# A hybrid attention layer on one core: sums of the mix and scalings of the first attention taken from GpSimd, and the residual loaded in four steps

## The chip, the cores and the metric

The program runs on one core of one Trainium2 chip. The metric is device time in microseconds (us) of one execution, the median of several runs. One execution of each kernel was taken by the hardware profiler as well. Its engines are PE (TensorE: matmuls, with PEld its weight loads), DVE (VectorE), ACT (ScalarE), POOL (GpSimd) and SP (which here only issues DMAs).

## The reference

One decoder layer for 512 tokens of width 1024, in float32. Two attentions run side by side on the same normed input and are mixed by gates; a convolutional gated MLP and a per-layer embedding follow.

```
h = rmsnorm(x); qa, ka, va, cq, ckv, kr, gates = split(h @ w_in)
ya = swa_attention(rope(qa), rope(ka), va, sinks)        # 8 heads, window 128
yb = mla_attention(...)                                  # 8 heads, dense causal
gate_a, gate_b = split(sigmoid(gates + b_gate))
mixed = gate_a * (ya @ w_branch_a) + gate_b * (yb @ w_branch_b)
x = x + rmsnorm(mixed @ w_out)
u_gate, u_val = split(causal_dwconv(rmsnorm(x) @ w_up))  # 2 x 2816 wide
x = x + rmsnorm((gelu(u_gate) * u_val) @ w_down)
x = x + sigmoid(rmsnorm(x) @ w_ple_gate) * (p @ w_ple)

# swa_attention, per block of 128 queries:
pr = exp(s - m) / (sum(exp(s - m)) + exp(sink - m));  out = pr @ v
```

## The kernel before

Every product is made of three matmuls on rounded halves of its operands: `split` (L71) writes a high part on ACT (`whi`, L72) and the rest on DVE (`wlo`, L73), and `mm3` (L75) multiplies high by high, high by low and low by high. A weight chunk of 128x1024 is thus loaded by SP's DMA queue into `wraw`, split on ACT and DVE, and used by PE (all matmuls carry line 56). PE has to wait for `whi` and `wlo` when these two engines are late.

The work goes in stages; times are those of the trace. Projections of the input (0 to 84 us); the first attention, in eight steps of a query block n and a head group g (`swa_scores` L493, `swa_pt` L527, `swa_pv` L549; to about 160); the second attention (`mla_scores` L562 and on; to about 250); the product with the first branch's weights (`psba`, 203 to 234); the mix, a loop over eight feature blocks m (L662 to L676; 248 to 279); w_out (`yo`) with its norm `post_norm` (L724); the up projection with the convolution (`pu`; 320 to 562); the down projection in two loops; the embedding and the last gate (`pe`, `pg`; 671 to 734). While the attentions run, `fill` (L479) puts matmuls of the gate projection (`psg`) between their steps, so that PE has work.

In one step of the first attention DVE takes the masked scores and their maximum out of PSUM, ACT takes four exponentials with their sums (`sw`, L518), DVE makes the reciprocal of the denominators (`den`, L522), POOL multiplies the whole step's `sw` by them in one instruction (L524), and PE transposes the result (`ptw`), which ACT and DVE split (`pwh`, `pwl`) for the product with v (`pvw`).

In the mix the four operations after the matmuls `pb` are

```
dve.scalar_tensor_tensor(ta, gb, 1.0, pb, ALU.add, ALU.mult)                # L673
pool.tensor_tensor(ta, ta, ga[:, m, :], ALU.add)                            # L674
act.activation(mxh[:, m, :], ta, AF.Copy, scale=0.5)                        # L675
dve.scalar_tensor_tensor(mxl[:, m, :], ta, 0.5, f32(mxh[:, m, :]), ...)     # L676
```

where `ta` is a block of the tile `gx` and `mxh`, `mxl` are the halves that `yo` uses.

The down projection takes 7 products for 8 blocks. The first loop (L899) over 11 chunks c fills `M1`, `M5`, `M7` and `M6`; `drain` (L936) sums them into `U`, `V12` (a part of a tile `T`) and `C22`; the second loop (L951) reloads half of each weight chunk, splits it, subtracts it from `T2[c]` (L958) for later, and goes on with `M1` and, one chunk behind, `M3`. Then `M4` uses the split `T2`. Before `drain`, POOL's queue loads the gain (`loadgain` L658) and the residual `xn` from DRAM in four parts of 512 KB (`load` L880, issued at L881); the `post_norm` of the MLP adds it at L736.

The program's order on each engine is made by a scheduler from the order in the code and priorities; `hot` (high priority) lifts a part of the code. Each engine then runs its instructions in that fixed order.

Of the kernel before, what the change touches and what calls it, by code (L numbers as in the profile page):

```python
# [8 lines left out]
F32 = mybir.dt.float32  # L9
F32R = mybir.dt.float32r  # L10
I32 = mybir.dt.int32
AF = mybir.ActivationFunctionType
ALU = mybir.AluOpType
PSUM = bass.MemoryType.PSUM

P = 128
S = 512
NB = 4
D = 1024
# [18 lines left out]
def hybrid_kernel(ctx, tc, T):  # L38
    nc = tc.nc
    act, dve, pool = nc.scalar, nc.vector, nc.gpsimd  # L40
    order = mybir.DependencyInfo(mybir.DependencyClass.NoSync, mybir.DependencyReason.DATA)

    class pe:
# [19 lines left out]
    def opened(**kw):  # L63
        cm = tc.tile_pool(reuse_waits="tile", **kw)
        p = cm.__enter__()
        return p, lambda: cm.__exit__(None, None, None)
# [38 lines left out]
    xp, close_xp = opened(name="xp", bufs=1, side="left")  # L105
# [6 lines left out]
    qkp, close_qkp = opened(name="qkp", bufs=1, side="right")  # L112
# [48 lines left out]
    def work(name="wkt"):  # L161
        return wk.tile([P, 1280], F32, name=name, tag="wkt", bufs=3)

    xh = xp.tile([P, 8, S], F32R, name="xh", tag="xh")
# [192 lines left out]
    qT = qkp.tile([P, 8, S], F32, name="qT", tag="qT")[:96]  # L357
# [10 lines left out]
    for n in range(NB):  # L368
        ps = scT("psqp")
        b = slice(n * P, (n + 1) * P)  # L370
        for k in range(2):
            w = slice(k * 256, (k + 1) * 256)
# [34 lines left out]
    ga = gap.tile([P, 8, S], F32, name="ga", tag="ga")  # L407
    gx = []

    def gate(m):  # L410
        return ga[:, m, :] if m < 8 else gx[(m - 8) // 3][:, (m - 8) % 3, :S]
# [29 lines left out]
    kT = qkp.tile([P, 8, S], F32, name="kT", tag="kT")[:96]  # L441
# [25 lines left out]
    def latent_kr():  # L467
# [4 lines left out]
        for h in range(1, 8):  # L472
# [4 lines left out]
                     e=latent_kr).get(t, lambda t=t: gates((int(t),)))() for t in ORDER.split()]  # L477
# [15 lines left out]
    def swa_scores(n, g):  # L493
        K = 256 if n else 128
        ks = slice(max(0, n - 1) * P, (n + 1) * P)
        mk = mswa if n else mswa[:, P:]
        b = slice(n * P, (n + 1) * P)
        s = work("sw")
        m, nm, sums, es = small("m"), small("nm"), small("sums"), small("es")
        for half in range(2):  # L500
            sc = scT("sc")
            for u in range(2):
                h = 4 * g + 2 * half + u
                o = sc[:, u * K:(u + 1) * K]
                pe.matmul(o, St[:, h, b], kh[:, g, ks], start=True, stop=False)
                pe.matmul(o, St[:, h, b], kl[:, g, ks], start=False, stop=True)
            for u in range(2):
                i = 2 * half + u
                h = 4 * g + i
                o = sc[:, u * K:(u + 1) * K]  # L510
                dve.tensor_tensor_reduce(
                    out=s[:, i * K:(i + 1) * K], in0=o, in1=mk, scale=0.125, scalar=sink[:, h:h + 1],
                    op0=ALU.add, op1=ALU.max, accum_out=m[:, i:i + 1])
        dve.tensor_scalar(nm, m, -1.0, None, ALU.mult)
        dve.tensor_tensor(es, sink[:, 4 * g:4 * g + 4], nm, ALU.add)
        for i in range(4):
            w = slice(i * K, (i + 1) * K)
            act.activation(s[:, w], s[:, w], AF.Exp, bias=nm[:, i:i + 1], accum_out=sums[:, i:i + 1])  # L518
        act.activation(es, es, AF.Exp)
        den = small("den")  # L520
        dve.tensor_tensor(den, sums, es, ALU.add)
        dve.reciprocal(den, den)  # L522
        sv = s[:, :4 * K].rearrange("p (i w) -> p i w", i=4)
        pool.tensor_tensor(sv, sv, den.unsqueeze(2).to_broadcast([P, 4, K]), ALU.mult)  # L524
        return s

    def swa_pt(n, g, s):  # L527
# [135 lines left out]
    for m in range(8):  # L663
        gb = gate(8 + m)
        if m % 2 == 0:
            ch_b = chunk(T["wbb"][m // 2])
        hi, lo = ch_b
        pb = p3[m]("pb")
        for k in range(4):
            w = slice((m % 2) * S + k * P, (m % 2) * S + (k + 1) * P)  # L670
            mm3(pb, hi[:, w], lo[:, w], ybT[0][:, k, :], ybT[1][:, k, :], k == 0, k == 3)
        ta = gb
        dve.scalar_tensor_tensor(ta, gb, 1.0, pb, ALU.add, ALU.mult)  # L673
        pool.tensor_tensor(ta, ta, ga[:, m, :], ALU.add)  # L674
        act.activation(mxh[:, m, :], ta, AF.Copy, scale=0.5)  # L675
        dve.scalar_tensor_tensor(mxl[:, m, :], ta, 0.5, f32(mxh[:, m, :]), ALU.mult, ALU.subtract)  # L676
    for f in (close_ca, close_wk, close_gap, close_sp, close_cqp, close_kvp, close_yp):
# [4 lines left out]
             raw=0, hi=0, lo=0)  # L682
# [75 lines left out]
    wx = [qkp.tile([P, 4, 1024], F32R, name="wx" + t, tag=t) for t in ("kT", "qT")]  # L758
# [14 lines left out]
    xd = [dp.tile([P, D], F32, name=f"xd{n}", tag=f"xd{n}") for n in range(NB)]  # L773
# [103 lines left out]

    loads = []

    def load(dst, src):  # L880
        i = pool.dma_start(dst, src).ins  # L881
        if loads:
            tc.add_manual_dep(i, loads[-1], order, reason="load order")
        loads.append(i.name)
# [4 lines left out]
    T2 = [T2t[c // 8][:, c % 8] for c in range(NC)]  # L889
    T13 = [T2t[1][:, 4 + 2 * i:6 + 2 * i].rearrange("p a t -> p (a t)") for i in range(2)]  # L890
    B1, B2 = slice(0, S), slice(S, 2 * S)
# [35 lines left out]
    open_res()  # L927
    xn = res["xn"]
    g_post = loadgain(T["mlp_post"], load, 1)
    for n in range(NB):  # L930
        load(xn[:, n, :], xd[n])
    Ut = vp.tile([P, 2, S], F32, name="U")
    C22t = ck.tile([P, 2, S], F32, name="C22", tag="t", bufs=3)
    U, C22 = ([t[:, b] for b in range(2)] for t in (Ut, C22t))
# [2 lines left out]
    def drain():  # L937
        for b in range(2):
            act.activation(U[b], M["M1"][b], AF.Copy)
            dve.tensor_tensor(U[b], M["M6"][b], U[b], ALU.add)  # L940
        for b in range(2):
            dve.tensor_tensor(V12[b], M["M5"][b], U[b], ALU.add)
            dve.tensor_tensor(U[b], M["M7"][b], U[b], ALU.add)
            dve.tensor_tensor(C22[b], M["M5"][b], U[b], ALU.add)
# [8 lines left out]
    for c in range(NC):  # L953
        raw = wtile("raw", F32)
        nc.sync.dma_start(raw, T["wd"][2 * c + 1])
        h, l = wtile("hi", F32R), wtile("lo", F32R)
        split(h, l, raw)
        dve.tensor_tensor(T2[c], raw[:, B1], T2[c], ALU.subtract)  # L958
        for b in range(2):
            t = slice(b * P, (b + 1) * P)  # L960
            lh, ll = p1[c][:, 0, 0, t], p1[c][:, 1, 0, t]
            for x, y in ((lh, h), (lh, l), (ll, h)):
                pe.matmul(M["M1"][b], x, y[:, B1], start=False, stop=c == NC - 1 and x is ll, skip_group_check=True)
        if late:
            m3(*late)
        late = (c, (h[:, B2], l[:, B2]))
# [6 lines left out]
    for c in range(NC):  # L973
        if c % 2 == 0:
            h, l = wtile("hi", F32R), wtile("lo", F32R)
        w = slice(c % 2 * S, (c % 2 + 1) * S)
# [3 lines left out]
    ph, pl = lA[:, 0:2], lA[:, 2:4]  # L980
    wpt = xp.tile([P, 4, D], F32R, name="wpt", tag="xl")
    wph, wpl = wpt[:, 0:2, :], wpt[:, 2:4, :]
    e = xp.tile([P, NB, D], F32, name="e", tag="xh")
    raw = wtile("raw", F32)
    nc.sync.dma_start(raw, T["pT"].rearrange("p a b -> p (a b)"))
    split(ph.rearrange("p a b -> p (a b)"), pl.rearrange("p a b -> p (a b)"), raw)
    for k in range(2):
        raw = wtile("raw", F32)
# [7 lines left out]
    for n in range(NB):  # L996
        b = slice(n * P, (n + 1) * P)
        for half in range(2):
            ps = bank(3 * (n % 2), "pe")
            w = slice(half * S, (half + 1) * S)  # L1000
# [5 lines left out]
        to_hT(n, xn[:, n, :], 1 + n // 2)  # L1006
    gp = lambda k: pp[:, PP_PLE + k:PP_PLE + k + 1]
    cg = [chunk(T["wpg"][k], g=gp(k)) for k in range(4)]
    wx = [qkp.tile([P, 4, 1024], F32R, name="wy" + t, tag=t) for t in ("kT", "qT")]
    cg += [chunk(T["wpg"][4 + k], g=gp(4 + k), dst=[t[:, k, :] for t in wx]) for k in range(4)]  # L1010
    lB = fp.tile([P, 4, S], F32, name="lB", tag="fB")
    outs = [0]
# [146 lines left out]
```

## Time and profile before

| | |
|---|---|
| time, median of 3 runs | 736.94 us (735.46 to 739.03) |
| time of the profiled execution | 735.66 us |
| its span, first to last instruction | 733.9 us |
| granted TensorE clock, mean | 1.000 |
| moved from and to HBM | 85.46 and 12.85 MB |

The span leaves 1.76 us of the profiled time outside. Of the views, the shares of busy time tell which engine is full, the waits tell what an engine waited for and how long, the chain shows the work that ended last followed back in time, and the timeline lists instructions with the idle time before them.

### The profile page before, as it was taken

To read this page: it belongs to the slowest core of one execution; us is meant where nothing else is said; L and a number is where in the kernel's file an instruction comes from. 1 tells how busy PE (TensorE), PEld (TensorE's weight loads), DVE (VectorE), ACT (ScalarE), POOL (GpSimd) and SP (SyncE) were. 2 spreads that over 40 slices of the span, in tenths; PEclk is the share of its full clock that TensorE was granted. 3 is DMA by queue.
4 is the path that set the end of the run, shared out by engine and by line. 5 is a ranking of instruction groups with operands and counts; after the bars stand their busy time and mean duration, and the time that the engine had idled before them with its cause. 6 is when DMAs were issued, how large, how long until landed. Compare 5 with 4: busy or idle time off the path is not lost.

```text
span 733.9 us, 9541 instructions
## 1 busy us (share of the span) xinstructions
PE 722.6 (98%) x3496; PEld 602.6 (82%) x3496; DVE 529.0 (72%) x935; ACT 363.3 (50%) x634; POOL 83.2 (11%) x99
## 2 busy tenths in 40 slices
PE   9999999999999999999999999999999999999997
PEld 9988877788778877899888888888888888788886
DVE  6567789986777486675777676687777987789632
ACT  5833577854553334446444443544544534268521
POOL 0104022100000062210000000000000322201000
PEclk9999999999999999999999999999999999999999
DMA  9611221112112226443434324334323798945111
GB/s 321 239 42 65 62 72 59 58 58 86 58 57 75 77 88 261 190 173 101 159 129 141 125 107 156 133 132 155 123 78 129 272 322 270 373 128 169 58 59 57
DMA packets 30814, 99.38 MB, mean 135 GB/s; under 512 B 4112, under 2 KB 5392, under 8 KB 30768
## 3 DMA queue, kind: packets, MB, share of 16 engines
q1 hardware_dynamic: 24960, 76.36, 31.4%
q0 software_dynamic: 5520, 22.02, 8.3%
q8 instruction: 27, 0.44, 0.3%
q10 hardware_dynamic: 288, 0.39, 0.2%
q14 instruction: 19, 0.16, 0.1%
HBM read 85.46 MB, written 12.85 MB: 134 GB/s over the span
## 4 chain that ended last, share of the span: by engine, by line
PE 90%; DVE 7%; issue 1%; DMA 1%; ACT 0%; DVEq 0%
PE pu L56 30%; PE M L56 13%; PE psg L56 11%; PE pg L56 6%; PE yo L56 5%; PE puh L56 3%; PE psba L56 3%; PE psA L56 3%; PE psB L56 2%; PE psC L56 2%; PE scm L56 2%; PE pe L56 2%; PE pb L56 1%; DVE wlo L73 1%; PE pvm L56 1%
## 5 line engine op out<-in xcount | busy, mean ns | idle before, releaser
L56 PE MATMUL pu<-hT,whi 128*128 128x512 f32 x640 | 197.0, 389 | 0.0
L72 ACT ACTIVATE whi<-wraw 128x1024 fp32r<-128x1024 f32 (+4 forms) x105 | 102.5, 976 | 168.0 <-PE pu L56 75.6
L73 DVE TENSOR_TENSOR wlo<-wraw,whi 128x1024 fp32r<-128x1024 f32 (+2 forms) x99 | 114.5, 1160 | 64.3 <-ACT whi L72 60.9
L56 PEld LDWEIGHTS pu<-hT,whi 128*128 128x128 f32 x640 | 120.1, 188 | 25.0
L56 PE MATMUL pu<-hT,wlo 128*128 128x512 f32 x320 | 124.5, 389 | 0.0
L56 PEld LDWEIGHTS pu<-hT,wlo 128*128 128x128 f32 x320 | 60.1, 188 | 12.4
L56 PE MATMUL psg<-xh,whi 128*128 128x512 f32 x128 | 51.1, 399 | 1.3 <-DVE ga L426 0.9
L56 PE MATMUL psg<-xl,whi 128*128 128x512 f32 x128 | 50.9, 398 | 0.0
L56 PE MATMUL psg<-xh,wlo 128*128 128x512 f32 x128 | 50.8, 397 | 0.0
L832 ACT ACTIVATE cv<-pu,pp 128x512 f32<-128x512 f32 x40 | 30.6, 765 | 9.1 <-PE pu L56 9.1
L72 ACT ACTIVATE whi<-T 128x512 fp32r<-128x512 f32 (+1 forms) x32 | 23.4, 761 | 21.2 <-DVE T L909 7.8
L833 DVE SCALAR_TENSOR_TENSOR cv<-pu,pp,cv 128x511 f32<-128x511 f32 x40 | 29.8, 746 | 3.1 <-ACT cv L832 3.1
L834 DVE SCALAR_TENSOR_TENSOR cv<-pu,pp,cv 128x510 f32<-128x510 f32 x40 | 29.9, 746 | 1.1
L674 POOL TENSOR_TENSOR gx<-gx,ga 128x512 f32<-128x512 f32 x8 | 15.3, 1929 | 132.7 <-DVE gx L673 132.7
L56 PEld LDWEIGHTS psg<-xh,whi 128*128 128x128 f32 x128 | 24.0, 188 | 7.1 <-DVE ga L426 1.1
L835 ACT ACTIVATE cv<-cv 128x512 f32<-128x512 f32 x22 | 13.9, 633 | 31.9 <-DVE cv L834 31.8
L73 DVE TENSOR_TENSOR wlo<-T,whi 128x512 fp32r<-128x512 f32 (+1 forms) x32 | 26.3, 851 | 3.3 <-ACT whi L72 3.3
L815 POOL DMA_DIRECT2D dd<-f2h x11 | 6.0, 546 | 198.7 <-ACT f2h L812 198.7
L56 PEld LDWEIGHTS psg<-xl,whi 128*128 128x128 f32 x128 | 24.1, 188 | 4.8 <-issue 0.2
L56 PEld LDWEIGHTS psg<-xh,wlo 128*128 128x128 f32 x128 | 24.1, 188 | 4.7
L56 PE MATMUL puh<-hT,whi 128*128 128x256 f32 x128 | 23.8, 285 | 0.1
L582 ACT ACTIVATE sm<-sm,nm 128x512 f32<-128x512 f32 (+3 forms) x32 | 17.6, 552 | 12.4 <-DVE nm L579 12.4
(324 smaller groups left out, 1640.8 us busy)
## 6 DMA issues: line engine op xcount, KB each, us to landing
wraw<-in_wup SPq DMA_DIRECT2D x44, 512.0 KB, 3.4
wraw<-in_wd SPq DMA_DIRECT2D x22, 512.0 KB, 4.3
wraw<-in_wg SPq DMA_DIRECT2D x16, 512.0 KB, 3.4
dd<-f2h POOLq DMA_DIRECT2D x11, 384.0 KB, 2.9
dd<-X POOLq DMA_DIRECT2D x11, 384.0 KB, 2.6
wraw<-in_wo SPq DMA_DIRECT2D x8, 512.0 KB, 3.6
wraw<-in_wpg SPq DMA_DIRECT2D x8, 512.0 KB, 3.8
wraw<-in_wd SPq DMA_DIRECT2D x11, 256.0 KB, 5.2
```

Source lines behind the costliest of these rows:

```text
L56: pe.chain(out, nc.tensor.matmul(out, *a, **k))
L72: act.activation(hi, src, AF.Copy)
L73: dve.tensor_tensor(lo, src, f32(hi), ALU.subtract)
L582: act.activation(s[:, w], s[:, w], AF.Exp, bias=nm[:, n:n + 1], accum_out=sums[:, n:n + 1])
L674: pool.tensor_tensor(ta, ta, ga[:, m, :], ALU.add)
L815: pool.dma_start(dd[c][:, i], f32(v))
L832: act.activation(c, u, AF.Identity, scale=w2, bias=cb)
L833: dve.scalar_tensor_tensor(c[:, 1:], u[:, :S - 1], w1, c[:, 1:], ALU.mult, ALU.add)
L834: dve.scalar_tensor_tensor(c[:, 2:], u[:, :S - 2], w0, c[:, 2:], ALU.mult, ALU.add)
L835: act.activation(cs[0], cs[0], AF.Gelu_apprx_tanh)
```

## The change

Five edits.

1. In `swa_scores` the one multiplication on POOL becomes four, one for each head of the group: two on ACT (Copy with a scale) and two on DVE.
2. In the mix the addition on POOL goes to DVE.
3. `drain` keeps its first half (the sums into `U` of `M1` and `M6`); the six other sums are written as `drain_rest`, called in the second loop at c = 2.
4. The four loads of `xn` no longer stand ahead of `drain`; each waits for the subtraction `T2[c]` of c = 2, 4, 6 and 8.
5. The tile `e` of the embedding moves to another buffer ("kT" for "xh"), and a half of the last gate's split weights takes "xh" in its place.

```
+    wait = mybir.DependencyInfo(mybir.DependencyClass.Sync, mybir.DependencyReason.DATA)
...
-        sv = s[:, :4 * K].rearrange("p (i w) -> p i w", i=4)
-        pool.tensor_tensor(sv, sv, den.unsqueeze(2).to_broadcast([P, 4, K]), ALU.mult)
+        for i in range(4):
+            w = slice(i * K, (i + 1) * K)
+            if i < 2:
+                act.activation(s[:, w], s[:, w], AF.Copy, scale=den[:, i:i + 1])
+            else:
+                dve.tensor_scalar(s[:, w], s[:, w], den[:, i:i + 1], None, ALU.mult)
...
-        pool.tensor_tensor(ta, ta, ga[:, m, :], ALU.add)
+        dve.tensor_tensor(ta, ta, ga[:, m, :], ALU.add)
...
-    def load(dst, src):
+    def load(dst, src, after=None):
         i = pool.dma_start(dst, src).ins
+        if after is not None:
+            tc.add_manual_dep(i, after, wait, reason="load pace")
...
-    for n in range(NB):
-        load(xn[:, n, :], xd[n])
...
             act.activation(U[b], M["M1"][b], AF.Copy)
             dve.tensor_tensor(U[b], M["M6"][b], U[b], ALU.add)
+
+    def drain_rest():
         for b in range(2):
             dve.tensor_tensor(V12[b], M["M5"][b], U[b], ALU.add)
             dve.tensor_tensor(U[b], M["M7"][b], U[b], ALU.add)
             dve.tensor_tensor(C22[b], M["M5"][b], U[b], ALU.add)
...
-        dve.tensor_tensor(T2[c], raw[:, B1], T2[c], ALU.subtract)
+        t4 = dve.tensor_tensor(T2[c], raw[:, B1], T2[c], ALU.subtract).ins.name
+        if c == 2:
+            drain_rest()
+        if c in (2, 4, 6, 8):
+            load(xn[:, c // 2 - 1, :], xd[c // 2 - 1], t4)
...
-    e = xp.tile([P, NB, D], F32, name="e", tag="xh")
+    e = qkp.tile([P, NB, D], F32, name="e", tag="kT")
...
-    wx = [qkp.tile([P, 4, 1024], F32R, name="wy" + t, tag=t) for t in ("kT", "qT")]
+    wx = [p.tile([P, 4, 1024], F32R, name="wy" + t, tag=t) for p, t in ((xp, "xh"), (qkp, "qT"))]
```

The orders below are those of the built programs. After the change the code stands some lines lower: L673, L676 and L73 of before are L678, L681 and L74.

DVE in the mix, before:

```order
L673 SCALAR_TENSOR_TENSOR gx_1630<-gx_1630,pb 128x512 x2
L73 TENSOR_TENSOR wlo<-wraw,whi 128x1024
L673 SCALAR_TENSOR_TENSOR gx_1630<-gx_1630,pb 128x512
L673 SCALAR_TENSOR_TENSOR gx_1631<-gx_1631,pb 128x512
L73 TENSOR_TENSOR wlo<-wraw,whi 128x1024
L676 SCALAR_TENSOR_TENSOR mxl<-gx_1630,mxh 128x512 x2
L673 SCALAR_TENSOR_TENSOR gx_1631<-gx_1631,pb 128x512
L676 SCALAR_TENSOR_TENSOR mxl<-gx_1630,mxh 128x512
```

DVE in the same place, after:

```order
L678 SCALAR_TENSOR_TENSOR gx_1654<-gx_1654,pb 128x512 x2
L74 TENSOR_TENSOR wlo<-wraw,whi 128x1024
L679 TENSOR_TENSOR gx_1654<-gx_1654,ga 128x512
L678 SCALAR_TENSOR_TENSOR gx_1654<-gx_1654,pb 128x512
L678 SCALAR_TENSOR_TENSOR gx_1655<-gx_1655,pb 128x512
L74 TENSOR_TENSOR wlo<-wraw,whi 128x1024
L679 TENSOR_TENSOR gx_1654<-gx_1654,ga 128x512 x2
L681 SCALAR_TENSOR_TENSOR mxl<-gx_1654,mxh 128x512
L679 TENSOR_TENSOR gx_1655<-gx_1655,ga 128x512
L678 SCALAR_TENSOR_TENSOR gx_1655<-gx_1655,pb 128x512
L681 SCALAR_TENSOR_TENSOR mxl<-gx_1654,mxh 128x512
```

The additions (L679) stand between the products of the gate with `pb`, and the `mxl` go in one at a time behind them; the splits of the weights keep their places among the products.

ACT in the first attention, before (the second row is the four exponentials of a step):

```order
L519 ACTIVATE es<-es 128x4
L518 ACTIVATE sw,sums<-sw,nm 128x256 x4
L519 ACTIVATE es<-es 128x4
L545 ACTIVATE yt<-pvw 64x4x128
L72 ACTIVATE whi<-wraw 128x512
L72 ACTIVATE pwh<-ptw 128x512
L451 ACTIVATE kT<-pskn 64x512
```

ACT in the same place, after:

```order
L520 ACTIVATE es<-es 128x4
L527 ACTIVATE sw<-sw,den 128x128 x2
L519 ACTIVATE sw,sums<-sw,nm 128x256 x4
L520 ACTIVATE es<-es 128x4
L527 ACTIVATE sw<-sw,den 128x256 x2
L550 ACTIVATE yt<-pvw 64x4x128
L73 ACTIVATE whi<-wraw 128x512
L527 ACTIVATE sw<-sw,den 128x256 x2
L73 ACTIVATE pwh<-ptw 128x512
```

The scalings (L527) stand in ACT's row ahead of the split of a weight chunk and of `pwh`, and each needs `den` from DVE.

DVE between the two loops of the down projection, before (L942 to L944 are the six later sums):

```order
L940 TENSOR_TENSOR U<-M_4959,U 128x512
L958 TENSOR_TENSOR T_4950<-wraw,T_4950 128x512
L942 TENSOR_TENSOR T_4951<-M_4954,U 128x512
L73 TENSOR_TENSOR wlo<-wraw,whi 128x1024
L958 TENSOR_TENSOR T_4950<-wraw,T_4950 128x512
L942 TENSOR_TENSOR T_4951<-M_4955,U 128x512
L943 TENSOR_TENSOR U<-M_4956,U 128x512
L958 TENSOR_TENSOR T_4950<-wraw,T_4950 128x512
```

DVE in the same place, after:

```order
L945 TENSOR_TENSOR U<-M_4983,U 128x512
L965 TENSOR_TENSOR T_4974<-wraw,T_4974 128x512
L949 TENSOR_TENSOR T_4975<-M_4978,U 128x512
L74 TENSOR_TENSOR wlo<-wraw,whi 128x1024
L965 TENSOR_TENSOR T_4974<-wraw,T_4974 128x512
L949 TENSOR_TENSOR T_4975<-M_4979,U 128x512
L950 TENSOR_TENSOR U<-M_4980,U 128x512
L965 TENSOR_TENSOR T_4974<-wraw,T_4974 128x512
```

The rows stand in the same order: the sums of `drain_rest` (L949, L950) are at the places that they had. In the order of POOL its DMAs are the same too, and SP's order is unchanged.

## Rows read from the trace of the kernel before

**Rows 1.** Page, part 1: engine, busy us, share of the span, instructions.
```profile
PE 722.6 (98%) x3496; PEld 602.6 (82%) x3496; DVE 529.0 (72%) x935; ACT 363.3 (50%) x634; POOL 83.2 (11%) x99
```

**Rows 2.** Waits of PE by releaser: us in all, times, longest.
```profile
PE pvw L56 <- ACT kT L451: 1.1, 1, 1.1
...
PE yo L56 <- DVE wlo L73: 1.0, 2, 0.7
...
PE pb L56 <- DVE wlo L73: 0.6, 1, 0.6
```

**Rows 3.** Windows: us; busy PE, PEld, DVE, ACT, POOL; PEclk, DMA share, GB/s.
```profile
100.00:123.00 23.00, 21.05 (x114) 16.74 (x113) 21.08 (x54) 16.19 (x44) 6.91 (x4) 1.00 0.16 50
260.00:279.00 19.00, 17.31 (x73) 13.01 (x72) 19.00 (x19) 8.46 (x11) 14.53 (x8) 1.00 0.27 84
622.00:637.00 15.00, 14.20 (x62) 11.38 (x62) 12.49 (x17) 4.36 (x5) 4.06 (x7) 1.00 0.94 337
637.00:672.00 35.00, 35.00 (x156) 28.39 (x156) 29.69 (x43) 23.00 (x38) 2.54 (x4) 1.00 0.53 171
```

**Rows 4.** Chain of the up projection: start us, us, what.
```profile
345.01 217.63 PE pu L56 x960
```

**Rows 5.** Timeline of PE in the mix: start us, us, instruction [idle before <-releaser].
```profile
261.29 1.21 PE L56 MATMUL pb<-ybT,whi 128*128 128x512 f32 x4
263.15 0.50 PE L56 MATMUL pb<-ybT,wlo 128*128 128x512 f32 x1 [0.64 <-DVE wlo L73]
...
277.54 0.39 PE L56 MATMUL yo<-whi,mxh 128*128 128x512 f32 x1
...
278.65 0.50 PE L56 MATMUL yo<-wlo,mxh 128*128 128x512 f32 x1 [0.72 <-DVE wlo L73]
```

**Rows 6.** Timeline of DVE in the mix.
```profile
259.95 1.28 DVE L673 SCALAR_TENSOR_TENSOR gx<-gx,pb 128x512 f32<-128x512 f32 x2 [2.80 <-PE pb L56]
261.16 1.94 DVE L73 TENSOR_TENSOR wlo<-wraw,whi 128x1024 fp32r<-128x1024 f32 x1
...
272.25 1.21 DVE L73 TENSOR_TENSOR wlo<-wraw,whi 128x1024 fp32r<-128x1024 f32 x1
273.38 1.77 DVE L676 SCALAR_TENSOR_TENSOR mxl<-gx,mxh 128x512 fp32r<-128x512 f32 x1
...
275.67 0.68 DVE L676 SCALAR_TENSOR_TENSOR mxl<-gx,mxh 128x512 fp32r<-128x512 f32 x1
```

**Rows 7.** Line groups: count | busy us, mean ns of one | idle before, releaser.
```profile
L674 POOL TENSOR_TENSOR gx<-gx,ga 128x512 f32<-128x512 f32 x8 | 15.3, 1929 | 132.7 <-DVE gx L673 132.7
L676 DVE SCALAR_TENSOR_TENSOR mxl<-gx,mxh 128x512 fp32r<-128x512 f32 x8 | 10.8, 1365 | 0.1
L587 DVE TENSOR_SCALAR sm<-sm,den 128x256 f32<-128x256 f32 x8 | 2.8, 347 | 0.0
```

**Rows 8.** Chain in the second attention.
```profile
143.56 1.07 DVE sm L587 x4
```

**Rows 9.** Line groups, ACT in the first attention.
```profile
L518 ACT ACTIVATE sw<-sw,nm 128x256 f32<-128x256 f32 x24 | 11.9, 500 | 2.4 <-DVE den L522 2.1 <-DVE nm L514 0.2
```

**Rows 10.** Timeline of DVE in the first attention.
```profile
115.73 2.51 DVE L73 TENSOR_TENSOR wlo<-wraw,whi 128x1024 fp32r<-128x1024 f32 x1
```

**Rows 11.** Timeline of PE between the two loops.
```profile
634.37 1.09 PE L56 MATMUL M<-whi,ffkT 128*128 128x512 f32 x4
...
636.26 0.50 PE L56 MATMUL M<-wlo,ffkT 128*128 128x512 f32 x1 [0.81 <-DVE wlo L73]
```

**Rows 12.** Chain between the two loops.
```profile
625.19 7.38 DMA wraw<-in_wd
```

**Rows 13.** Timeline of POOL, same stretch.
```profile
625.65 2.11 POOL L881 DMA_DIRECT2D xn<-xd  x4
659.28 1.40 POOL L732 TENSOR_TENSOR q<-q,mhalf 128x1 f32<-128x1 f32 x2 [31.52 <-DVE q L731]
```

**Rows 14.** Timeline of DVE, same stretch.
```profile
632.59 0.69 DVE L958 TENSOR_TENSOR T<-wraw,T 128x512 f32<-128x512 f32 x1 [1.35 <-DMA wraw<-in_wd]
```

## The prediction

> **What bounds the kernel now.** First the shares of busy time: PE is busy 98% of the span [rows 1]; the up projection runs 960 matmuls back to back at 217.63/960 = 0.2267 us each [rows 4]. The edits touch no matmul, so they can only win where PE stands still. Second the waits of PE: the releasers that the edits concern are DVE's splits of the weights (`wlo`), 0.6 us before `pb` and 1.0 us in two waits before `yo`; none of the rows read there has POOL as the releaser [rows 2]. Third the windows, stage by stage [rows 3]: in the mix (260 to 279) DVE is busy for all of the 19.00 us while PE has 19.00 − 17.31 = 1.69 idle; in the first attention (100 to 123) DVE is busy 21.08 of 23.00 and PE 21.05; between the down loops (622 to 637) PE lacks 0.80, with DMA at 0.94; from 637 to 672 PE is full. So the bound is PE, and behind it, in these three places, DVE or a load. All that can be won there is some 5 us of 736.
>
> All sums are made against the profiled execution, 735.66 us, which lies 1.28 us below the median of 736.94; the forecast adds the 1.28 back. A measurement of this kernel can tell about 0.5%, 3.7 us, from no change.
>
> **The addition in the mix (edit 2).** I read what PE loses from start to start, with 0.2267 us for each matmul. Four matmuls from 261.29 end at 262.20, the next starts at 263.15: 0.95 lost. One from 277.54 ends at 277.77, the next starts at 278.65: 0.88 lost [rows 5]. The other wait of `yo` is 1.0 − 0.7 = 0.3 [rows 2]. Together 2.1 us, all for a `wlo` that DVE makes late.
>
> Why is it late? DVE's `mxl` takes 1.77 us once and 0.68 another time, the same instruction with the same sizes; a `wlo` takes 1.94 and then 1.21 [rows 6]. The mean `mxl` is 1.365, and in this stage POOL runs eight additions of 1.929 each [rows 7], 14.53 us of the 19.00 [rows 3]. I take the long ones to be those that lie beside an addition on POOL. [...]
>
> With the edit DVE gets eight additions. The nearest row is two products of the same tile that take 1.28 together, so 1.28 − 0.68 = 0.60 from one to the next [rows 6]: +4.8 us. It loses 8 × (1.365 − 0.68) = 5.5 us on `mxl` and 1.94 − 1.21 = 0.7 on a `wlo`. So DVE has 1.4 us less to do, not more, and the chain from the product to `mxl` has 0.68 in place of POOL's 1.93. More matters the order: up to the fourth `wlo` of the stage DVE now has 18 short instructions and 4 splits, 18 × 0.60 + 4 × 1.15 = 15.4 us (1.15 is a split's step where splits follow each other, 1.21 less the overlap of 0.06). From 259.95 that is 275.3, where PE wants it at 277.77. The ends are 0 (all additions stand where they delay the same split) and −2.1; I take **−2.1**, since the slack of 2.4 us is larger than the losses.
>
> **The scalings of the first attention (edit 1).** Eight instructions on POOL go; ACT gets 16 and DVE 16, of 256 columns (four of each of 128). The trace has the same DVE instruction in the second attention: 0.347 us by its duration [rows 7], 4 in 1.07, 0.27 from one to the next [rows 8]. 16 × 0.27 = +4.3 us for DVE. It gets back what it lost beside POOL: the longest split there took 2.51 [rows 10] against 1.21 [rows 6], −1.3. Net +3.0. POOL ran four of its instructions in the full window of 100 to 123 [rows 3], half of all; so 8 × 0.27 − 1.3 = +0.9 falls there. On ACT one costs about the 0.500 of an exponential of that size [rows 9], 16 × 0.5 = 8 us at most, on an engine that is busy 16.19 of those 23 us; it stands in order ahead of `pwh` and of weight splits and waits for `den`, so what is late next is a split on ACT, and then PE's transposes and `pvw`. The ends: −2.0, the whole 23.00 − 21.05 of PE, if the shorter way to `ptw` and the new order of PE's steps close its gaps; +3.0 if all of DVE's net load lands on PE. I take **+0.9**, nearest to the window's row, where DVE is 92% full.
>
> [...]
>
> **Between the loops (edits 3 and 4).** PE's four matmuls from 634.37 should end at 635.28; the next starts at 636.26, 0.98 lost [rows 11]. It waited for a `wlo`, that stood behind the sums, those behind a `T2` that idled 1.35 us for a load [rows 14], and that load took 7.38 us [rows 12]. At the same time POOL's queue moved the gain and four residual parts, issued from 625.65 on [rows 13]; the stretch moves 337 GB/s with DMA at 0.94 [rows 3]. The subtraction at 632.59 is that of c = 5. After, the first part can start as before (c = 2 lies three chunks earlier), the second only after c = 4, and two come behind c = 5, after the stretch in question. Two parts are 1.05 MB, at 337 GB/s 3.1 us, more than the 1.35 that DVE idles. The sums of `drain_rest` stand in DVE's row where they stood, so edit 3 by itself moves nothing there: 0, covered by the unchanged order. Term: **−1.0**. Ends: −1.0 and, if one of the later parts holds a weight load up in its turn, 524 KB/337 GB/s = +1.6; against this speaks that DMA is at 0.53 there and PE full [rows 3]. Each part's wait blocks POOL's queue behind it, but its next work is at 659.28, 31.52 us after the last issue [rows 13]; a chunk there is 12 matmuls, 2.7 us, so c = 8 comes some 8 us after 632.59 or, with PE's pace from 636, up to 644, and the residual is added behind that power of 659.28. Cover: 15 us; without it the norm would wait for the part's landing.
>
> **The buffers (edit 5).** 0: PE is full in the stage before [rows 3]; the earlier or later split of weights is hidden by its matmuls. If the exchange made `e` wait for an old reader, some 0.5 us would show at `pe`.
>
> **The sum:** −2.1 + 0.9 − 1.0 = −2.2; 735.66 − 2.2 = 733.5 for a profiled execution, **734.7** on the median's scale.
>
> **The rivals.**
> - **The attention's gaps close too.** PE's idle in 100 to 123 has its largest wait not on POOL but on `kT` of ACT, 1.1 [rows 2], and steps that are ordered anew can miss it. Then −2.0 in place of +0.9: 734.7 − 2.9 = 731.8. For it: the order of ACT and PE there changes throughout. Against it: DVE is nearly full.
> - **The scalings land on PE.** All +3.0 in place of +0.9: 736.8. For it: 92% on DVE and the waits in order on ACT. Against it: `fill` has gate matmuls in between.
> - **Slower: `mxl` is long for a reason of its own.** If the 1.77 do not come from POOL's additions, the eight additions make a full engine fuller: +4.8 in place of −2.1, 741.6. It decides as soon as the mean `mxl` after stays above 1.365 − 0.60 = 0.77 us, and has its full price at 1.365. Against it: the same instruction took 0.68 in the same stage [rows 6].
> - **The pacing brings nothing,** because the load is late for another reason (its own buffer's release): 734.7 + 1.0 = 735.7.
>
> **How the numbers follow.** Chances: the forecast's case 0.43 (its own range 733.0 to 736.2), the gaps close 0.26, the scalings land on PE 0.17, the pacing brings nothing 0.08, the slower rival 0.06. The likeliest gives 734.7. The range runs from 730.7, the first rival with about 1 us for the scatter of a median of few runs, to 738.5, the second with 1.7 for a split held up on ACT; outside lie the slower rival, and tails of 0.1. Faster by over 0.5% means below 733.3: nearly all of the first rival and a tail of the forecast's case, 0.33. Slower means above 740.6: the last rival and a small tail of the second, 0.08. Between them 0.59.
>
> **What would show it.** In the mix: `mxl` near 0.68 in all eight, DVE's additions near 0.68, no wait of PE on `wlo` there. In the attention: the busy share of DVE in 100 to 123 as high as before and no 2.5 us split; PE's idle there around 2 to 3 us. Between the loops: no DVE idle on `wraw` ahead of the sums and no PE wait at the sixth chunk; the residual landed before the norm's power at some 657. It would be wrong if `mxl` stayed long, if PE waited for `pwh`, `ptw` or a weight split in the attention by more than 3 us, or if a new wait came up from 637 to 672.

## The result and the profile after

The changed kernel takes 741.07 us (median of 6 runs, 739.78 to 741.99) against 735.87 us of the kernel before in the same runs: a ratio of 1.0062, 95% interval 1.0040 to 1.0083. (The ratios here are those on record, formed over all runs; the quotient of two medians comes near them but is not the same, here 1.0071.) It is slower by 0.6%, where 734.7 us was forecast. The profiled execution took 740.39 us, 4.73 more than that of before.

The page's shares of busy time of the changed kernel, against [rows 1]:

```profile
PE 724.8 (98%) x3496; PEld 604.9 (82%) x3496; DVE 529.7 (72%) x959; ACT 369.4 (50%) x650; POOL 59.6 (8%) x83
```

POOL lost 23.6 us of work, DVE's sum is what it was (the 24 new instructions are paid by shorter ones) and ACT has 6 more. PE is busy 2.2 us longer with the same 3496 matmuls. What PE waits for has changed, against [rows 2] (waits of PE by releaser: us in all, times, longest):

```profile
PE scm L57 <- DVE m L581: 2.7, 2, 1.6
PE puh L57 <- ACT hT L758: 1.5, 1, 1.5
PE sc L57 <- DVE m L512: 1.4, 1, 1.4
...
PE M L57 <- DVE wlo L74: 0.6, 1, 0.6
PE ptw L61 <- DVE pwl L74: 0.6, 1, 0.6
```

The waits of `pb` and `yo` on `wlo` are gone. In their place stand three waits in the attention (`scm` and `sc` for `m`, with which DVE frees a bank of scores; `ptw`) and one of the up projection's first matmuls (`puh`) on ACT's `hT`. The windows show where, against [rows 3] (us; busy PE, PEld, DVE, ACT, POOL; PEclk, DMA share, GB/s):

```profile
100.00:123.00 23.00, 20.99 (x107) 17.07 (x107) 20.22 (x59) 19.44 (x52) 0.00 (x0) 0.93 0.15 48
123.00:146.00 23.00, 20.31 (x92) 15.10 (x91) 20.47 (x60) 16.42 (x45) 0.00 (x0) 0.99 0.22 70
...
260.00:279.00 19.00, 18.98 (x82) 15.12 (x82) 15.02 (x22) 7.44 (x10) 0.00 (x0) 1.00 0.35 112
...
637.00:672.00 35.00, 34.43 (x149) 27.61 (x148) 29.20 (x41) 19.83 (x30) 3.13 (x4) 1.00 0.58 199
```

For 123 to 146, which [rows 3] does not have, the kernel before shows

```profile
123.00:146.00 23.00, 22.75 (x104) 16.86 (x103) 20.45 (x59) 17.71 (x48) 3.79 (x2) 1.00 0.22 69
```

In the mix PE now stands still for 0.02 us of 19.00, where it was 1.69, and DVE is busy 15.02 instead of all the time. In the first attention PE's busy time falls from 22.75 to 20.31 in 123 to 146. In 100 to 123 it hardly changes (20.99 for 21.05), but there a second number has changed that the forecast left out: the granted clock, 1.00 before, is 0.93, and PE's row holds 107 matmuls where it held 114. The 0.57 us that PE lacks in 637 to 672 are the old wait for `wlo` between the loops, which lies some 4 us later now.

The engines' share of the mix, in the line groups (count | busy us, mean ns | idle before, releaser):

```profile
L681 DVE SCALAR_TENSOR_TENSOR mxl<-gx,mxh 128x512 fp32r<-128x512 f32 x8 | 5.3, 685 | 0.5 <-ACT mxh L680 0.5
L679 DVE TENSOR_TENSOR gx<-gx,ga 128x512 f32<-128x512 f32 x8 | 5.3, 684 | 0.0
```

All eight `mxl` take 685 ns where their mean was 1365 [rows 7]: without POOL's additions beside them the extra time is gone, as read.

To add up the parts I took, for each matmul of PE, the time to the start of the next one and subtracted the median that its shape has in the kernel before. What is over is PE's loss, summed by the stage of the matmul that came late; in brackets the part of it that belongs to matmuls started while the clock was granted at 0.5. Us, of one profiled execution each:

| stage | before | after | edit 1 alone | edit 2 alone | edits 3 to 5 alone | edits 2 to 5 |
|---|---|---|---|---|---|---|
| attentions | 5.95 | 11.02 (3.29) | 9.22 (1.52) | 6.07 | 5.99 | 5.99 |
| mix and w_out | 3.39 | 1.38 | 3.49 | 1.08 | 3.37 | 1.07 |
| up projection | 0.08 | 1.96 | 0.08 | 1.96 | 0.08 | 3.43 (1.43) |
| down projection | 2.96 | 2.69 | 2.83 | 3.38 | 2.89 | 2.55 |

For the change these are +5.1, −2.0, +1.9 and −0.3, together 4.7, the difference of the two profiled executions. Of the +5.1 in the attentions, 3.3 is lost at the low clock and only 1.8 is longer gaps.

### The profile page after: what moved, and what is told of

It is laid out like the page before. It is cut to its first block, busy times and chain, and to the rows that moved or that the text cites. A ratio compares the mean times of both kernels' runs of the same rounds, so it can differ in the third digit from the quotient of the medians.

```text
span 738.6 us, 9537 instructions
## 1 busy us (share of the span) xinstructions
PE 724.8 (98%) x3496; PEld 604.9 (82%) x3496; DVE 529.7 (72%) x959; ACT 369.4 (50%) x650; POOL 59.6 (8%) x83
## 4 chain that ended last, share of the span: by engine, by line
PE 85%; DVE 8%; DMA 5%; ACT 2%; issue 1%; ACTq 0%; DVEq 0%
PE pu L57 29%; PE psg L57 11%; PE pg L57 6%; PE yo L57 6%; DMA wraw<-in_wd 5%; PE M L57 5%; PE puh L57 3%; PE pb L57 3%; PE psA L57 3%; PE psba L57 3%; DVE wlo L74 3%; PE psB L57 2%; PE psC L57 2%; PE scm L57 2%; PE pe L57 2%; PE pvm L57 1%
## 5 line engine op out<-in xcount | busy, mean ns | idle before, releaser
L73 ACT ACTIVATE whi<-wraw 128x1024 fp32r<-128x1024 f32 (+4 forms) x105 | 102.4, 976 | 167.2 <-PE pu L57 76.9
L74 DVE TENSOR_TENSOR wlo<-wraw,whi 128x1024 fp32r<-128x1024 f32 (+2 forms) x99 | 111.8, 1132 | 73.2 <-ACT whi L73 67.8
L73 ACT ACTIVATE whi<-T 128x512 fp32r<-128x512 f32 (+1 forms) x32 | 23.4, 760 | 20.9 <-PE M L57 11.9
L74 DVE TENSOR_TENSOR wlo<-T,whi 128x512 fp32r<-128x512 f32 (+1 forms) x32 | 26.3, 852 | 1.9 <-ACT whi L73 1.9
L737 POOL TENSOR_TENSOR q<-q,mhalf 128x1 f32<-128x1 f32 x8 | 5.9, 746 | 257.2 <-DVE q L736 257.0
L57 PE MATMUL puh<-hT,whi 128*128 128x256 f32 x128 | 23.6, 285 | 1.7 <-ACT hT L758 1.5
L57 PE MATMUL scm<-kT,qT 96*128 96x512 f32 (+3 forms) x64 | 20.1, 446 | 2.7 <-DVE m L581 2.7
```

Source lines behind the costliest of these rows:

```text
L57: pe.chain(out, nc.tensor.matmul(out, *a, **k))
L73: act.activation(hi, src, AF.Copy)
L74: dve.tensor_tensor(lo, src, f32(hi), ALU.subtract)
L737: pool.tensor_tensor(r1, v, mhalf[:, :1], ALU.pow)
```

## The experiments

### Each edit by itself

The first four runs take the edits apart; the diffs are those of the change, each alone.

**Edit 1 alone** (four scalings on ACT and DVE in place of POOL's one).

> The kernel before with edit 1 alone (scalings on ACT and DVE). Theory: the whole loss of the change comes from the first attention, where PE's gaps grow by about 2 us and the granted clock falls to 0.50 behind two of them, some 2.5 us more; so +4 to +6 us against before, gaps before sc and scm, clock below 1.0 in 100 to 150, and no gap ahead of puh. Rival (no part of the loss is of edit 1 by itself, it takes the order that all edits together make): within 1.5 us of before, clock 1.000.

Measured: 740.36 against 735.80 us, ratio 1.0051 (1.0034 to 1.0069). The loss is of edit 1 by itself; its waits are those of the changed kernel in the attention, and nothing is lost ahead of `puh`. Of its 12 executions, the only one with a mean clock of 1.000 took 738.11.

**Edit 2 alone** (the mix's addition).

> The kernel before with edit 2 alone (the mix's addition on DVE). Theory: -2.0 us in the mix, and +1.7 back where PE ends yo, transposes and waits for ACT's hT ahead of puh, since its transposes stand behind all of yo in this order as in the changed kernel; so -0.5 to +0.3 us in sum, clock 1.000. Rival (the gap ahead of puh belongs to another edit): -1.7 to -2.3 us.

Measured: 736.70 us, ratio 0.9995 (0.9978 to 1.0011). By the table it wins 2.3 us in the mix and w_out and loses 1.9 at the up projection: a win that is given back 40 us later.

**Edits 3 to 5 alone.**

> The kernel before with edits 3, 4 and 5 alone (sums later, residual paced, buffers exchanged). Theory: the pacing shortens the load's wait and PE's loss ahead of the wlo between the loops falls from 0.97 to about 0.7, so -0.2 to -0.5 us. Rival (the forecast: the whole loss goes): -1.0 us.

Measured: 736.02 us, ratio 1.0003 (0.9984 to 1.0022). PE's loss in the down projection is 2.89 for 2.96: nothing that can be told from no change. By PE's rows both expectations were too high; the interval of the time, −1.2 to +1.6 us, could not tell the smaller one from none.

**Edits 2 to 5**, the changed kernel without edit 1.

> The changed kernel with edit 1 undone (scaling on POOL again). Theory: the attention is as before, clock 1.000, so 5 us faster than the changed kernel; against before -0.3 to -0.9 us, being -2.0 in the mix, +1.7 ahead of puh, -0.3 between the loops. Rival (the loss is of the order that all edits together make): still +3 us or more against before.

Measured: 736.27 us, ratio 1.0002 (0.9978 to 1.0027). The attention is as before (5.99). PE's losses add up to more than was expected, for a reason that the next part shows; the interval of the time, −1.6 to +2.0 us, would have room for the expectation too.

### The wait ahead of the up projection, and the clock

Why does edit 2 lose at `puh`? In the kernel before, the 16 transposes (`ptr`) of the first two token blocks stand in PE's row among the matmuls of `yo`, at 312.66, with the last 23 matmuls of `yo` behind them; in the order with edit 2 they stand behind the last matmul of `yo`. The timeline of the changed kernel (start us, us, instruction [idle before <-releaser]):

```profile
320.84 1.91 PE L61 MATMUL ptr<-ident,t 128*128 128x128 f32 x16
...
321.48 1.09 ACT L758 ACTIVATE hT<-ptr 128x512 fp32r<-128x512 f32 x2 [4.60 <-PE ptr L61]
...
324.26 0.50 PE L57 MATMUL puh<-hT,whi 128*128 128x256 f32 x2 [1.51 <-ACT hT L758]
```

Transposes, ACT's two copies and DVE's differences now come one after the other while PE has nothing else. The gap is the same with edit 2 alone and with edits 2 to 5, to the hundredth of a microsecond; but the stretches behind it are not. First edit 2 alone, its wait and two windows:

```profile
319.02 0.50 PE L56 MATMUL puh<-hT,whi 128*128 128x256 f32 x2 [1.51 <-ACT hT L753]
...
321.00:323.00 2.00, 2.00 (x19) 2.00 (x18) 1.86 (x3) 0.11 (x1) 1.26 (x1) 1.00 0.11 39
323.00:325.00 2.00, 2.00 (x19) 2.00 (x18) 1.35 (x2) 1.43 (x3) 1.06 (x3) 1.00 0.32 129
```

and edits 2 to 5:

```profile
319.55 0.50 PE L57 MATMUL puh<-hT,whi 128*128 128x256 f32 x2 [1.51 <-ACT hT L754]
...
321.00:323.00 2.00, 2.00 (x13) 2.00 (x12) 2.00 (x4) 0.02 (x1) 0.73 (x1) 0.58 0.30 117
323.00:325.00 2.00, 2.00 (x12) 2.00 (x12) 1.56 (x2) 1.15 (x2) 1.33 (x2) 0.56 0.06 25
```

PE is busy all the time in both, with 19 matmuls in 2 us in the one and 12 or 13 in the other: the clock was granted at 0.5 for (0.42 + 0.44) x 2.00/0.5 = 3.4 us, and cost 1.43. So a gap of PE can have a price behind it that it has in one execution and not in another; in the profiled execution of the changed kernel, too, the same gap has no fall behind it. How often the clock falls in the timed executions is not shown. Their mean clock was below 0.999 in all 12 of edits 2 to 5 and in 17 of the 35 of the kernel before, but the times of those 17 (median 736.3 us) lie close to those of the other 18 (735.7), and the last 0.7 us of the profiled span of before are at the low clock as well, where no matmul is left to be held up (PE's last one ends at 729.5).

**The transposes early.** To test the order by itself, the changed kernel got one constraint more:

```
             to_hT(0, ts[0])
+            ptrs[2] = pe.newest
             to_hT(1, ts[1])
+            ptrs[3] = pe.newest
...
-    def half_pass(ps, half, blocks, chunks, lh, ll):
+    def half_pass(ps, half, blocks, chunks, lh, ll, first={}):
...
         for c, (hi, lo) in enumerate(chunks):
+            pe.behind = first.get(c)
```

The matmuls of chunk c of the last block's second half (`first` is `ptrs` there) are ordered behind the transposes that `pe.behind` names.

> The changed kernel with one order more: the transposes of the first two token blocks (ptr) stand ahead of the third and of the last quarter of the last block's second half of yo. Theory: the gap of 1.67 and 0.38 ahead of puh goes, and with it a fall of the clock behind it in some executions; -1.5 to -3 us against the changed kernel, so +2 to +4 against before. Rival (hT is late anyway, since its input t is): no change, +5 against before, the gap stands ahead of the transposes.

Measured: 739.10 against 736.51 us, ratio 1.0036 (1.0023 to 1.0049), so by the ratios 0.26% or 1.9 us less than the change's own 1.0062, with intervals that overlap. PE's loss ahead of `puh` falls from 1.96 to 1.14. So the order made this wait, and the constraint takes away 0.8 us of it; what is left are waits for DVE's `hT` (0.5 in two) and `q` (0.2). The rest of the 1.9 is not the transposes': in this execution the attentions lose 9.96 for 11.02, with one fall of the clock in place of two.

**Edits 2 to 5 with the transposes early.**

> Edits 2 to 5 without edit 1, with the transposes early as in the run on them. Theory: the mix's 2.0 and 0.3 between the loops remain and nothing is given back: -2 to -2.6 us against before, PE's losses in 300 to 340 under 0.8 and the clock 1.000 there. Rival: as without that order, 0 to +0.5 us.

Measured: 734.60 us, ratio 0.9975 (0.9952 to 0.9999), −1.8 us, and the clock 1.000 there: PE loses 1.13 ahead of `puh` where edits 2 to 5 lost 3.43. Edit 2's win stays for the most part when its order doesn't give it back, though the interval ends close to no change.

### What the scalings cost in the attention

The windows of the changed kernel just behind its wait of `sc` at 105.75 show the clock again:

```profile
106.00:108.00 2.00, 1.37 (x10) 0.99 (x10) 1.97 (x7) 0.52 (x2) 0.00 (x0) 0.99 0.53 203
108.00:110.00 2.00, 2.00 (x8) 1.60 (x8) 1.94 (x5) 1.74 (x3) 0.00 (x0) 0.50 0.36 131
110.00:112.00 2.00, 2.00 (x7) 1.61 (x6) 1.99 (x8) 1.98 (x8) 0.00 (x0) 0.65 0.03 8
```

A second fall comes at about 145.5, behind a wait of `scm`. There DVE's row can be read, first of the changed kernel:

```profile
139.90 1.23 DVE L74 TENSOR_TENSOR wlo<-wraw,whi 128x1024 fp32r<-128x1024 f32 x1
...
141.56 1.27 DVE L592 TENSOR_SCALAR sm<-sm,den 128x512 f32<-128x512 f32 x4
...
142.75 0.68 DVE L581 CUSTOM_DVE_ANT_0 sm<-scm,cst 128x512 f32<-128x512 f32 x1
...
143.49 3.08 PE L57 MATMUL scm<-kT,qT 96*128 96x512 f32 x8 [1.59 <-DVE m L581]
```

and then of the kernel before:

```profile
140.04 0.69 DVE L576 CUSTOM_DVE_ANT_0 sm<-scm,cst 128x512 f32<-128x512 f32 x1
...
141.69 1.22 DVE L73 TENSOR_TENSOR wlo<-wraw,whi 128x1024 fp32r<-128x1024 f32 x1
...
143.56 1.26 DVE L587 TENSOR_SCALAR sm<-sm,den 128x512 f32<-128x512 f32 x4
```

PE wants a bank of scores that DVE now takes out at 142.75, behind a weight split and the scalings of the second attention; before, the scores came first and those two behind them. The last of the new instructions stand at 131.4 (DVE) and 134.3 (ACT), 8 us and more ahead of it: with them the scheduler has made another order for the whole attention, in which PE reaches the scores sooner than DVE does. At the first place it is alike: pvw's two products, which filled a part of the gap before, stand behind `sc` and `ptw` now, and the gaps from 104 to 108 grow from 2.1 to 2.5 us; there it is the fall of the clock that costs, 1.65 us of the 3.29. Does it matter on which engine the work is put?

**All scalings on DVE**, the edit alone with `i < 0` for `i < 2`, and **all on ACT**, with `i < 4`.

> The kernel before with edit 1 alone, all 32 scalings on DVE (16 more there, none on ACT). Theory A (the loss of edit 1 comes from ACT's row, where scalings that wait for den stand ahead of pwh and of weight splits): less loss than edit 1 alone, 0 to +2 us against before. Theory D (it comes from DVE's load, since PE's longer gaps ahead of scm end with DVE's m): more, 32 x 0.27 = 8.6 us on DVE, +6 to +9 us.

> The kernel before with edit 1 alone, all 32 scalings on ACT. Theory A: more loss than edit 1 alone, 32 x 0.45 = 14 us on ACT, +6 to +10 us. Theory D: less, 0 to +2 us, the gap ahead of scm back at 0.3.

Measured: 744.20 against 736.51 us, ratio 1.0105 (1.0086 to 1.0124), and 736.67 us, ratio 1.0002 (0.9986 to 1.0018). That is what theory D (DVE's load) expected, but the stages say otherwise. The windows of 100 to 146 and the largest waits of PE, first all on DVE, then all on ACT, which has a window of the mix as well:

```profile
100.00:146.00 46.00, 41.90 (x192) 31.30 (x191) 41.41 (x115) 29.99 (x78) 0.00 (x0) 0.97 0.21 70
...
PE M L56 <- DVE wlo L73: 2.4, 1, 2.4
PE ptw L60 <- DVE pwl L73: 2.3, 2, 1.5
```

```profile
100.00:146.00 46.00, 42.25 (x209) 33.21 (x208) 39.16 (x111) 42.10 (x114) 0.00 (x0) 0.96 0.18 59
...
260.00:279.00 19.00, 19.00 (x85) 15.73 (x85) 17.85 (x18) 8.46 (x11) 13.90 (x8) 1.00 0.24 84
...
PE pvw L56 <- DVE yt L551: 2.4, 3, 1.5
PE psg L56 <- DVE qT L464: 1.8, 1, 1.8
PE ptw L60 <- DVE pwl L73: 1.5, 1, 1.5
```

PE is busy some 42 of 46 us in both and the clock falls in both. PE's losses in the attentions are 11.06 us (1.50 of it at the low clock) with all on DVE and 9.70 (1.53) with all on ACT, 5.1 and 3.8 above before. What tells the two totals apart lies outside the attentions. With all on DVE, PE loses 4.90 us in the mix and w_out where it lost 3.39, and 6.08 in the down projection where it lost 2.96 (the wait of 2.4, with a fall of the clock behind it that costs 1.42). With all on ACT it loses 0.35 in the mix and w_out, with the additions still on POOL and a mean `mxl` of 1155 ns: in this order the weight splits come in time all the same. So the totals agreed with theory D for a wrong reason, and neither theory stands: in the attentions the scalings cost 4 to 5 us on either engine. What PE waits for there is DVE each time, but not the same result: the scores' `m` with the change, `pwl` and, for 1.1 us, `m` with all on DVE, `yt`, `qT` and `pwl` with all on ACT.

**The load alone.** The next two keep POOL's scaling, and so the way from the exponentials to the transposes, and add to each step two instructions whose result nobody reads, in one run on ACT, in the other on DVE:

```
         pool.tensor_tensor(sv, sv, den.unsqueeze(2).to_broadcast([P, 4, K]), ALU.mult)
+        for i in range(2):
+            act.activation(s[:, 1024:1024 + K], mswa[:, :K], AF.Copy, scale=den[:, i:i + 1])
...
+            dve.tensor_scalar(s[:, 1024:1024 + K], mswa[:, :K], den[:, i:i + 1], None, ALU.mult)
```

> The same with the 16 additional instructions on ACT (Copy of a constant mask scaled by den, 500 ns each for 256 columns). Theory L: +1 to +4 us. Theory C: 0 to +0.7 us. If only one of the two engines shows a loss, that engine's row was the cause of edit 1's gaps.

Measured: 738.55 against 736.09 us, ratio 1.0023 (1.0006 to 1.0041). The attentions lose 8.97 us (1.82 at the low clock), about what edit 1 alone does, though nobody reads the added work. Its largest wait of PE, and what DVE did ahead of that:

```profile
PE sc L56 <- DVE m L511: 2.5, 1, 2.5
...
101.61 0.16 DVE L521 TENSOR_TENSOR den<-sums,es 128x4 f32<-128x4 f32 x1 [2.78 <-ACT es L519]
...
102.62 2.50 DVE L73 TENSOR_TENSOR wlo<-wraw,whi 128x1024 fp32r<-128x1024 f32 x1
```

and in the kernel before:

```profile
101.13 0.16 DVE L521 TENSOR_TENSOR den<-sums,es 128x4 f32<-128x4 f32 x1 [1.97 <-ACT es L519]
...
103.05 1.59 DVE L73 TENSOR_TENSOR wlo<-wraw,whi 128x1024 fp32r<-128x1024 f32 x1
```

DVE idles 2.78 us for ACT's last exponential where it idled 1.97, and its split then falls beside POOL's scaling and takes 2.50 where it took 1.59. So with 16 instructions of half a microsecond on ACT the attentions lose 3.0 us more, 1.8 of it at the low clock, which is what theory L asked for. But of the largest gap some 0.9 us (2.50 − 1.59) is the longer split beside POOL's scaling, which edit 1 cannot have, and this kernel has an order of its own as well; so it is not shown that the load alone is enough.

> The kernel before, POOL's scaling kept, with 16 more instructions on DVE in the first attention, two per step, of the form and size of edit 1's scalings: they multiply a constant mask by den into a spare part of the step's tile, and nobody reads them. Theory L (what costs is the place that 16 instructions take in a nearly full engine's row): +2 to +4 us against before, PE's losses in the attention up by 2 us or more. Theory C (what costs is that the scaling itself, on the way to the transposes, now waits in such a row): 0 to +0.7 us.

Measured: 752.26 us, ratio 1.0202 (1.0171 to 1.0233), far more than theory L asked for. The run has a second cost that edit 1 does not have; the line's summary (min/median/max ns), and DVE's and POOL's timeline:

```profile
L526 DVE TENSOR_SCALAR sw<-cst,den x16: 276/354/1867, 89.0 to 147.6; 128x256 f32<-128x256 f32 x12, 128x128 f32<-128x128 f32 x4
...
100.40 2.25 DVE L526 TENSOR_SCALAR sw<-cst,den 128x256 f32<-128x256 f32 x2
...
100.53 1.97 POOL L524 TENSOR_TENSOR sw<-sw,den 128x1024 f32<-128x1024 f32 x1 [1.26 <-DVE den L522]
```

Beside POOL's scaling a pair of these takes 2.25 us where a pair of edit 1's takes 0.62; the longest single one takes 1867 ns against a median of 354, about the 1.97 us of POOL's instruction. So this run does not price DVE's load by itself.

### The loads between the loops

The changed kernel's chain between the loops, against [rows 12], and its parts of the residual in POOL's timeline, against [rows 13]:

```profile
629.65 7.44 DMA wraw<-in_wd
```

```profile
630.42 0.55 POOL L886 DMA_DIRECT2D xn<-xd  x1
634.70 0.53 POOL L886 DMA_DIRECT2D xn<-xd  x1 [3.74 <-DVE T L965]
642.77 0.53 POOL L886 DMA_DIRECT2D xn<-xd  x1 [7.54 <-DVE T L965]
647.44 0.53 POOL L886 DMA_DIRECT2D xn<-xd  x1 [4.14 <-DVE T L965]
```

The pacing works, but the weight load is no shorter: 7.44 us, and 7.42 with edits 3 to 5 alone, against 7.38. Over all traces it took 7.35 to 8.35 us in the seven runs without edit 4 and 7.15 to 7.84 in the five with it. The next run took the gain and the residual away from it:

```
-    g_post = loadgain(T["mlp_post"], load, 1)
...
-        if c in (2, 4, 6, 8):
-            load(xn[:, c // 2 - 1, :], xd[c // 2 - 1], t4)
+        if c == 5:
+            g_post = loadgain(T["mlp_post"], lambda d, s: load(d, s, t4), 1)
+        if c in (6, 7, 8, 9):
+            load(xn[:, c - 6, :], xd[c - 6], t4)
```

> Edits 3 to 5 alone, with the gain and all four parts of the residual later: the gain waits for the subtraction of c = 5, the parts for c = 6, 7, 8 and 9. Theory (the weight load of 7.4 us shares the DMA engines with whatever POOL's queue has in transit, the gain and one part being enough, so that the pacing of edit 4 takes nothing from it): with the queue empty the load takes under 5.5 us, DVE's idle ahead of the sums and PE's 0.95 there go, -0.7 to -1.1 us. Rival (the weight loads limit themselves): load 7 us or more, no change.

Measured: 735.35 against 736.09 us, ratio 0.9986 (0.9968 to 1.0003). The chain, PE's wait, and what POOL's queue still issues there:

```profile
624.98 6.58 DMA wraw<-in_wd
...
PE M L57 <- DVE wlo L74: 0.3, 1, 0.3
...
623.79 0.70 POOL L882 DMA_DIRECT2D fffA<-dd  x1 [4.19 <-PE M L57]
624.49 0.72 POOL L882 DMA_DIRECT2D fffB<-dd  x1
```

With nothing of the gain or the residual beside it the load takes 6.58 us, and 6.96 in the last run below: shorter than in any of the twelve other traces, but not under 5.5. So the gain and the residual hold it up by some 0.4 to 0.8 us against 7.38. The queue is not empty, as the theory wanted it: `fffA` and `fffB` still land at 629.45 and 630.92, beside the load, as they do in the kernel before. Whether they or the weight loads themselves make up the rest was not tried.

### A version that beats both

The last run takes edits 2, 3 and 5, POOL's scaling, the transposes another quarter earlier, and the later loads.

> Edits 2, 3 and 5, the scaling on POOL as before, the transposes one quarter earlier than in the runs on them, gain and residual later as in the run on it. Theory: -1.9 in the mix and yo, ahead of puh 0.2 to 0.4 in place of 1.1, -0.9 between the loops: -2.5 to -3.5 us against before, clock 1.000. Rival: one of the moves makes a new wait, the transposes for their input (a gap ahead of ptr) or the norm for the residual (a gap after M4): -1.5 or less.

Measured: 734.29 against 736.09 us, ratio 0.9964 (0.9950 to 0.9979), −2.7 us by the ratio and −1.8 by the medians, faster than both kernels. The weight load between the loops, and the waits that are left in these places:

```profile
623.96 6.96 DMA wraw<-in_wd
...
PE M L60 <- DVE wlo L77: 0.7, 1, 0.7
PE puh L60 <- DVE q L736: 0.6, 1, 0.6
```

The mix and w_out keep their 2.0. Ahead of `puh` 1.12 is still lost, no less than with the transposes one quarter later, and between the loops 0.7 of PE's wait is there again in this execution. So it gives the mix's win and little else.

## Why the prediction was wrong

The forecast added up −2.1 for the mix, +0.9 for the scalings, −1.0 between the loops and 0 for everything else. PE's rows gave −2.0, +5.1, −0.3, and +1.9 ahead of the up projection, a place that the forecast left out.

**Bound, and the mix: right.** PE stands still only in a few places, the splits were late because `mxl` and `wlo` ran beside POOL's additions (1365 and 1420 ns in the mean, 685 and 1219 without them), and the addition costs DVE 0.68. The term of −2.1 measured −2.0 to −2.3 in PE's rows (mix and w_out). The rival that ended on the other side fell with `mxl` at 685 ns. One thing the step did not see: with all scalings on ACT the additions stay on POOL, `mxl` and `wlo` stay long (1155 and 1606 ns in the mean), and PE loses only 0.35 there. So slow splits cost PE only in an order that puts them late, and how much of the 2.0 is the freed DVE and how much the new order is not shown.

**The scalings: the term was mis-sized, and its upper end too low.** "+0.9 falls there" with ends of −2.0 and +3.0 measured +5.1 in the profiled execution, and edit 1 alone +0.51% (0.34 to 0.69) of the time, 2.5 to 5.1 us. Two things were left out. The step counted DVE's net load in the window, and took ACT's 16 instructions as hidden on an engine at 16.19 of 23.00; it left out that in a new order PE can come to a result of DVE's before DVE has made it. With the change these are the scores, 4.1 us of waits on `m`; in all three ways to place the scalings off POOL the attentions' loss grows by 3 to 5 us. And every gap was priced at its own length: the clock that falls behind it cost 1.4 to 1.7 us more each time, and fell twice in the profiled execution, 3.3 of the 5.1. The rival "the scalings land on PE" was the nearest, with too low a price, 736.8. How much of edit 1's gaps is load and how much is the order that the scheduler happens to make stays open, as each variant gets an order of its own.

A part of the size was right: a scaling takes 348 ns on DVE and 494 on ACT in the changed kernel, as read from [rows 7, 9]. With edit 1 alone DVE is busy 531.2 us for 529.0; what is lost beyond these 2.2 is waits and the clock.

**A term was missing.** The forecast named the first three places where PE loses time and looked in the new order at these alone. The order of PE where `yo` ends had changed as well, the transposes behind 23 matmuls that they had stood ahead of, and it was costed at nothing by not being read. It cost 1.9 us, and with edits 2 to 5 a fall of the clock that cost 1.43 more; moving it back gave 0.8 by PE's rows in the changed kernel, and 2.3 with edits 2 to 5, where the fall went too.

**Between the loops: −1.0 measured −0.3, within what two executions differ by.** The step "two parts are 1.05 MB, at 337 GB/s 3.1 us, more than the 1.35 that DVE idles" failed. It took all four parts to be moving at once beside the weight load. The parts stand in one queue behind the gain: in the kernel before the load landed at 632.57, the gain at 633.14 and the parts one by one at 635.14 to 639.54. So the two that edit 4 takes away moved after the load anyway, and the gain and the first part stay beside it. Even without these it took 6.58 and 6.96 us.

**Edit 5: right at 0;** the tail's loss is 0.79 for 0.68.

Of the profile's signs that were named, `mxl` and the mix came as said. The sign of a wrong forecast, waits for `pwh`, `ptw` or a weight split of more than 3 us in the attention, did not come in these words: 4.7 us of waits came there, but 4.1 of them on the scores' `m` and 0.6 ahead of `ptw`.

## What to carry to other kernels

Where a scheduler makes the order, read PE's new order to the end and not only around the edit: a win in one stage may move work that fed the next one, and one constraint can bring a part of it back. Moving work off an idle, slow engine paid in the mix (an addition took 1929 ns on POOL and 684 on DVE), where it freed the full engine of more than it added (DVE was busy 19.00 us of the stage's 19.00 and is now busy 15.02); in the attention it added to rows that were nearly full (DVE at 21.08 of 23.00 us), and cost more than any sum of busy times said. A total that agrees with a theory can do so for another reason, as that of all scalings on ACT did: ask which stage it comes from. And a gap of PE costs more than its length when the clock falls behind it, by 1.4 to 1.8 us a fall in these traces.

## What the runs showed of the hardware

- The granted clock fell to 0.5 for about 3.4 us behind gaps of PE, at a price of 1.4 to 1.8 us per fall by PE's rows (9 falls in seven traces; with the load on DVE two falls lasted 6.8 us and cost 3.2 each). The same gap (1.51 us of wait ahead of `puh`, in the same order) was followed by a fall in one profiled execution and by none in two others.
- A scaling of 256 columns on DVE takes 348 ns alone and up to 1867 beside POOL's instruction; on ACT 494 ns, and in the run with POOL's scaling beside it 511 at most.
- The weight load between the loops took 7.35 to 8.35 us in seven traces where POOL's queue was given the gain and four parts beside it, 7.15 to 7.84 in five with the gain and one part, later two, and 6.58 and 6.96 in two with neither.
